# Two-layer hybrid diffusion step on one core: the differential parts' transfers on GpSimd's queue, four of layer 1's first tiles on VectorE, and a planned order chosen by its mean end over varied lengths

## The chip, the core and the metric

One core of one Trainium2 chip runs the kernel. The metric is device time in microseconds (us) of one execution; less is better. TensorE is called PE, VectorE DVE, ScalarE ACT, GpSimd POOL and SyncE SP, as in the profile. SP computes nothing here: it issues most of the DMA transfers. A DMA instruction can also stand in ACT's or POOL's own stream. Each engine carries out its own stream strictly in order, so an instruction that waits holds everything behind it on that engine.

## The reference

A trunk of two layers is applied to 128 context tokens and 256 latent tokens with the same weights. Cut to what matters:

```python
def _mixer_front(x, mod, lp):
    h = _rms(x, lp['g_mix']) * (1.0 + mod[1]) + mod[0]
    cq, ckv, krope, na_q, na_k, na_v, df_q, df_k, df_v = _split_in(h @ lp['w_in'])
    ...
def _diff_attend(q, k, v, lp, lam_init):          # 4 heads of two 32-wide halves
    s1 = q[..., :32] @ k[..., :32].T * scale; s2 = q[..., 32:] @ k[..., 32:].T * scale
    p = softmax(s1) - lam * softmax(s2)
    return _rms(p @ v, lp['g_df_sub']) * (1.0 - lam_init)
def _finish(x, o_mla, o_na, o_df, mod, lp):
    x = x + mod[2] * (concat(o_mla, o_na, o_df) @ lp['w_out'])
    h = _rms(x, lp['g_ffn']) * (1.0 + mod[4]) + mod[3]
    return x + mod[5] * ((silu(h @ lp['w_gate']) * (h @ lp['w_up'])) @ lp['w_down'])
```

`mod` is `silu(cond) @ w_mod + b_mod`, six rows of 1024 for each kind of token. D_MODEL is 1024, the inner width of the last block (the FFN) 2816. Everything is float32.

## The kernel before, in words

**Tiling.** The 384 tokens stand as columns: `xT` is 8 tiles of 128 features by 384 tokens. Float32 accuracy comes from splitting each operand into a high and a low part: `split_hi` (ACT, line 291, tile `wh`) and `split_lo` (DVE, line 297, tile `wl`) make the two parts of a weight block, and `mm3` (lines 363 to 365) runs three PE matmuls for each product. A weight block arrives by a DMA on SP into one of three `raw` buffers (lines 281 and 318).

**Stages.** Each layer has a planned stage (adaLN, norm, input projection `g1`, the three attentions, and the first part of the output projection) and then a plain stage (rest of the output projection and the FFN), where PE gets weight after weight. Between the layers stands a short norm. In the planned stage, the gate rows of `mod` are made beside the attention: `ModSet.load` (line 404) fetches 1 MB of `w_mod` into a `raw` buffer by SP, and `ModSet.mm` (line 414, tile `m`) multiplies it on PE.

**First tiles.** At the start of a layer the 8 feature tiles are normalised: `norm_mul` (DVE, line 552, tile `nt`), `norm_aff` (line 560: two instructions, latent and context tokens) on POOL for the tiles `k` in `POOLK[l]` and else on DVE, `norm_hi` (ACT, line 556, `hh`) and `norm_lo` (DVE, line 564, `hl`). The input projection needs `hh` and `hl` tile by tile.

**Differential heads.** `done_d(p)` takes a 128-token block of a pair of heads: squares, a sum, `rsqrt` on POOL (lines 583 and 584), scaling, rotation (tile `dfo`), a PE transposition (line 1344), and the high and low part in `hs`. `away` (line 1354) writes `hs` to the DRAM tensor `parts`, one DMA of 512 rows of 512 bytes. When the three blocks of a pair are there, `spread` (line 1398) in `df_unit(h)` reads them back for head `h` in eight DMAs of 32 partitions each, in the order of parts that the split product needs, into the tiles `qu` and `ku`. The score matmuls (line 1083) of that head need all eight. So a layer has 6 `away` and 4 `spread`, and all 12 and 64 of these DMAs stand in SP's stream. The neighbourhood heads have a POOL instruction too: a MEMSET (line 1106) of the unused columns of the tile `e`, which the PE transposition (line 1050) of `e` waits for.

**What sets the order.** In the planned stage nothing is ordered by hand. `Plan.add` records tasks with an engine, a cost in us, predecessors, buffers and a priority; `Plan.order` plays them through on these costs and starts on each engine the ready task of best priority. `Plan.best` tries `ORDERS` sets of disturbed priorities, keeps the one whose last task ends first, and the tasks are written to the engines' streams in order of their start. A task on the engine `"dma"` is one in SP's stream, with `LAG` added until its data are there. The plain stage is written in program order.

Of the kernel before, what the change touches and what calls it, by code (L numbers as in the profile page):

```python
# [12 lines left out]
F32 = mybir.dt.float32  # L13
# [5 lines left out]
P = 128  # L19
DM = 1024  # L20
KD = DM // P
NT = 384
# [14 lines left out]
OUT_EARLY = 3  # L37
BUB = (1, 2, 3)
AHEAD = 1
POOLK = ((1, 3, 5, 7), (0, 2, 3, 4, 5, 6, 7))  # L40
PARTS = 4
PARAM = (28, 11)
LAG = 2.8
# [10 lines left out]

WARMUP = (18, 0.43, 16)

ORDERS, STIR = 300, 3.0
CYCLE = 'zszstzt'
WARM = 1
PRT, PRO = (-4.0, -1.1)  # L60
# [24 lines left out]
class Task:  # L85
    def __init__(self, eng, dur, fn, take, prio, ready, lag=0.0):
        self.eng, self.dur, self.fn, self.take, self.prio, self.ready, self.lag = eng, dur, fn, take, prio, ready, lag
        self.need, self.then, self.frees, self.users, self.held, self.start, self.dense = 0, [], [], 0, [], None, 0


class Plan:
# [5 lines left out]
    def __init__(self, room, dense, warm):  # L97
        self.room, self.dense, self.tasks, self.warm = dict(room), dense, [], warm

    def add(self, eng, dur, fn, after=(), take=(), frees=(), prio=0.0, ready=0.0):  # L100
        t = Task(eng, dur, fn, take, prio, ready, LAG if eng == 'dma' else 0.0)
        self.tasks.append(t)
        for a in after:
            if a is not None:
                a.then.append(t)
                t.need += 1
        for h in frees:
            h.users += 1
            t.frees.append(h)
        return t  # L110

    def best(self):

        tasks, room, dense = self.tasks, dict(self.room), self.dense
        was = [(t.need, t.users, t.ready) for t in tasks]

        def run(prios):
            for t, (t.need, t.users, t.ready), t.prio in zip(tasks, was, prios):
                t.held = []
            self.room, self.dense = dict(room), dense  # L120
            return self.order()
        draw = random.Random(0)
        base = [t.prio for t in tasks]
        free = [i for i, t in enumerate(tasks) if t.dur and t.eng != "room"]
        best = list(base)
        run(best)
        end = self.end
        for _ in range(ORDERS):
            p = list(best)
            for i in draw.sample(free, draw.choice((1, 2, 4, 8, 16, 40))):  # L130
                p[i] = base[i] + draw.gauss(0, STIR if draw.random() < 0.8 else 5 * STIR)
            try:
                run(p)
            except AssertionError:
                continue
            if self.end <= end:
                end, best = self.end, p
        return run(best)

    def fit(self, t):  # L140

# [10 lines left out]
    def order(self):  # L152
        events, free, now, n = [], {}, 0.0, 0
        ready = {}
        window, busy, warm = 0, {i: WINDOW for i in range(WARM)} if self.warm else {}, self.warm
        for i, t in enumerate(self.tasks):
            t.key = (t.prio, i)
            free[t.eng] = 0.0
            if not t.need:
                ready.setdefault(t.eng, []).append(t)  # L160
        left = len(self.tasks)
        while left:
            for e in free:
                while free[e] <= now:
                    for t in sorted((t for t in ready.get(e, ()) if t.ready <= now), key=lambda t: t.key):
                        got = self.fit(t)
                        if got is not None:
                            break
                    else:
                        break  # L170
                    ready[e].remove(t)
                    for r in got:
                        self.room[r] -= 1
                    dur = t.dur
# [12 lines left out]
                    t.held, t.start = got, now  # L187
                    free[e] = now + dur
                    n += 1
                    if t.lag:  # L190
                        heapq.heappush(events, (now + dur, -n, t, "wake"))
                    heapq.heappush(events, (now + dur + t.lag, n, t, "done"))
                    heapq.heappush(events, (now + dur + t.lag + self.HOP, n, t, "free"))
            times = [x.ready for l in ready.values() for x in l if x.ready > now]
            if events:
                times.append(events[0][0])
            assert times, [(t.eng, t.take, t.prio, t.fn.__qualname__.split(".")[-1]) for l in ready.values() for t in l][:20]
            now = max(now, min(times))
            while events and events[0][0] <= now:
                _, _, t, what = heapq.heappop(events)  # L200
                if what == "done":
                    left -= 1
                    self.end = now
                    for u in t.then:
                        u.need -= 1
                        u.ready = max(u.ready, now + (0.0 if u.eng == t.eng else self.HOPS.get((t.eng, u.eng), self.HOP)))
                        if not u.need:
                            ready.setdefault(u.eng, []).append(u)
                    self.dense -= t.dense
                elif what == "free":  # L210
                    for h in t.frees:
                        h.users -= 1
                        if not h.users:
                            for r in h.held:
                                self.room[r] += 1
        return sorted(self.tasks, key=lambda t: t.start)


@with_exitstack
def trunk(ctx: ExitStack, tc, xT_d, cv_d, crow_d, pcol_d, prow_d, cache_d, dfk_d, rope_d, bias_d, ident_d,  # L220
# [439 lines left out]
    for l in range(DEPTH):  # L660
# [141 lines left out]
            parts = [None]  # L802
        for k in range(KD):
            x = {}
            a = add(DVE, 0.47, lambda k=k, x=x: x.update(t=norm_mul(k, nst["row"][:, :NT])), after=[bcs], take=("row",), frees=[bcs], prio=URGENT / 2 + k)
            on_pool = k in POOLK[l]
            b = add(POOL if on_pool else DVE, 1.08 if on_pool else 0.6, lambda k=k, x=x, e=nc.gpsimd if on_pool else nc.vector: norm_aff(l, k, x["t"], e),
                    after=[a, parts[k * len(parts) // KD]], prio=NORMP + k)
            b = add(ACT, 0.42, lambda k=k, x=x: norm_hi(k, x["t"], hh), after=[b], prio=NORMP + k)
            hready[k] = add(DVE, 0.47, lambda k=k, x=x: norm_lo(k, x["t"], hh, hl), after=[b], frees=[a], prio=NORMP + k)  # L810

        def weights(key, lead=None, prio=-1000.0, pairs=None):

# [8 lines left out]
            elif lead is None:  # L822
                n = rs[0] * rs[1]
                if pairs:
                    lead = add(DMA, 2.95 / 4096 * n, lambda: w_raw(rk, src, rs, 0), take=("raw", "graw"), prio=pairs[0])
                    lead.mate = add(DMA, 2.95 / 4096 * n, lambda: w_raw(rk, src, rs, 1), after=[lead], prio=pairs[1])
                else:
                    lead = add(DMA, 2.95 / 2048 * n, lambda: w_raw(rk, src, rs), take=("raw", "graw"), prio=5.0 + len(plan.tasks))
            n = shape[0] * shape[1]
# [467 lines left out]
        def done_d(p):  # L1297
            hd = slice(2 * p, 2 * p + 2)

            def done(t, z, unit, room):  # L1300
# [50 lines left out]
                    nc.vector.tensor_tensor(x["hs"][:, 1], x["pt"], x["hs"][:, 0].bitcast(F32), op=ALU.subtract)  # L1351

                def away():
                    nc.sync.dma_start(parts_d[p][:, :, :, t * P:(t + 1) * P], x["hs"].bitcast(F32))
                pr = PDD
                a = add(ACT, 0.27, copy, after=[unit], take=("tok",), frees=[room], prio=URGENT / 2)
                vd_ready[p].append(add(ACT, 0.17, vals, after=[unit], frees=[room], prio=URGENT / 2))
# [9 lines left out]
                g = add(PE, 0.23, turn, after=[f], take=("t",), frees=[f], prio=pr)  # L1367
                u = add(ACT, 0.3, high, after=[g], take=("hs",), frees=[g], prio=pr)
                v = add(DVE, 0.33, low, after=[u], frees=[g], prio=pr)
                df_ready[p][t] = add(DMA, 0.7, away, after=[v], frees=[u], prio=pr)  # L1370
            return done

        du = {}
# [1 line left out]
        def df_unit(h, after, pr):  # L1375
# [17 lines left out]
            def spread():  # L1393

                src = parts_d[h // 2][64 * (h % 2):64 * (h % 2) + 64]
                for i, order in enumerate(((0, 1, 1, 0), (0, 0, 1, 1))):
                    for j, w in enumerate(order):
                        nc.sync.dma_start(du[h][i][32 * j:32 * j + 32, :, (0, P)[i]:(0, P)[i] + NT].bitcast(F32),
                                          src[:, w, i].rearrange("(a r) t -> r a t", a=2))
# [422 lines left out]
```

## Time and profile before

| | |
|---|---|
| median of 3 runs | 1003.67 us (1001.21 to 1004.65) |
| the profiled execution | 1002.43 us, of which the span from first to last instruction is 1000.6 us |
| PE busy | 981.8 us (98%) |
| DVE, ACT, POOL busy | 710.2, 492.9, 153.5 us |
| layer 0 planned stage | from 0 to about 240 us |
| layer 0 plain stage | to about 514 us |
| layer 1 planned stage | about 516 to 720 us |
| layer 1 plain stage | to the end |

How to read it: PE is the engine that matters. "Busy" counts a matmul from start to end, and matmuls overlap, so the places where PE's time is lost are looked for as idle time of PE in stretches of the span, as waits of PE, and in the chain that ended last. The granted TensorE clock is given as a share of full speed.

### The profile page before, as it was taken

The numbers are of one execution on the slowest core, as the hardware profiler recorded it, in microseconds if no ns is written. First come the engines' busy times: TensorE is split into PE (matmuls) and PEld (weight loads), VectorE is DVE, ScalarE is ACT, GpSimd is POOL, SyncE is SP. The second block draws the span as 40 slices with busy tenths as digits, with TensorE's granted clock in tenths as the row PEclk, the third lists the DMA queues.
The fourth block names the chain that finished last, engine by engine and source line by source line (L and its number), as shares of the span: only waits on it lengthen the run. The fifth ranks groups of instructions, "written<-read, shape, count | busy, mean of one in ns | idle before, by whom it ended". The sixth has DMA issues, their size and how long they took to land.

```text
span 1000.6 us, 16452 instructions
## 1 busy us (share of the span) xinstructions
PE 981.8 (98%) x6002; PEld 920.6 (92%) x6002; DVE 710.2 (71%) x1625; ACT 492.9 (49%) x1121; POOL 153.5 (15%) x239
## 2 busy tenths in 40 slices
PE   8999998999999999999999999999999999999998
PEld 7877777999999999999978877889999999999998
DVE  4678876986999999964356887788789655553332
ACT  3366776875433333333326666786653344332221
POOL 2165211201000010100015621230010000000000
PEclk9999999999999999999999999999999999999999
DMA  9858665336666657684462365431765434334450
GB/s 358 334 185 259 215 195 175 109 111 232 201 220 193 228 184 227 200 284 133 134 207 86 109 193 155 137 122 55 253 207 167 132 115 138 102 112 124 137 153 26
DMA packets 139664, 172.84 MB, mean 173 GB/s; under 512 B 6337, under 2 KB 118593, under 8 KB 137281
## 3 DMA queue, kind: packets, MB, share of 16 engines
q1 hardware_dynamic: 131168, 143.38, 45.2%
q0 software_dynamic: 6832, 27.77, 8.1%
q8 instruction: 47, 0.77, 0.3%
q10 hardware_dynamic: 1584, 0.66, 0.2%
q14 instruction: 33, 0.26, 0.1%
HBM read 165.59 MB, written 6.19 MB: 172 GB/s over the span
## 4 chain that ended last, share of the span: by engine, by line
PE 89%; ACT 3%; DMA 2%; DVE 2%; POOL 2%; issue 1%; SPq 0%; ACTq 0%; DVEq 0%; POOLq 0%
PE z L363 13%; PE z L364 13%; PE z L365 13%; PE t L363 6%; PE t L364 6%; PE t L365 6%; PE s L363 6%; PE s L364 6%; PE s L365 6%; PE s L1083 3%; PE m L414 2%; PE t L1050 2%; DMA raw<-in_w_mod 2%; PE t L1191 1%; POOL nt L560 1%; PE s L957 1%
## 5 line engine op out<-in xcount | busy, mean ns | idle before, releaser
L291 ACT ACTIVATE wh<-raw 128x768 fp32r<-128x768 f32 (+3 forms) x224 | 203.3, 909 | 363.5 <-PE z L364 136.0
L297 DVE TENSOR_TENSOR wl<-raw,wh 128x768 fp32r<-128x768 f32 (+3 forms) x224 | 232.5, 1038 | 113.2 <-ACT wh L291 112.2
L363 PE MATMUL z<-fh,wh 128*128 128x386 f32 x304 | 103.2, 339 | 0.0
L364 PE MATMUL z<-fl,wh 128*128 128x386 f32 x304 | 103.0, 339 | 0.0
L365 PE MATMUL z<-fh,wl 128*128 128x386 f32 x304 | 102.6, 338 | 0.0
L486 DVE CUSTOM_DVE_ANT_0 sums<-wt,sums,pcol 128x1024 f32<-128x1024 f32 x80 | 102.3, 1278 | 0.3 <-DVE small L1654 0.3
L363 PE MATMUL z<-wh,hh 128*128 128x384 f32 (+1 forms) x264 | 102.1, 387 | 0.3 <-ACT tok L876 0.3
L365 PE MATMUL z<-wh,hl 128*128 128x384 f32 (+1 forms) x264 | 90.3, 342 | 1.4 <-DVE hl L564 1.4
L364 PE MATMUL z<-wl,hh 128*128 128x384 f32 (+1 forms) x264 | 90.1, 341 | 0.0
L584 POOL TENSOR_TENSOR small<-small,mhalf 128x4 f32<-128x4 f32 (+4 forms) x58 | 72.7, 1254 | 4.8
L363 PE MATMUL s<-fh,wh 128*128 128x386 f32 x200 | 68.2, 341 | 0.0
L363 PE MATMUL t<-fh,wh 128*128 128x386 f32 x200 | 68.1, 341 | 0.0
L364 PE MATMUL s<-fl,wh 128*128 128x386 f32 x200 | 67.8, 339 | 0.0
L364 PE MATMUL t<-fl,wh 128*128 128x386 f32 x200 | 67.8, 339 | 0.0
L365 PE MATMUL t<-fh,wl 128*128 128x386 f32 x200 | 67.5, 338 | 0.0
L365 PE MATMUL s<-fh,wl 128*128 128x386 f32 x200 | 67.5, 338 | 0.0
L1109 ACT ACTIVATE e<-s,small 128x384 f32<-128x384 f32 (+2 forms) x110 | 54.4, 500 | 14.5 <-DVE small L1094 13.0
L480 POOL DMA_DIRECT2D wt<-in_w_modT x40 | 21.6, 540 | 245.7 <-DVE mod L486 190.0
L364 PEld LDWEIGHTS z<-fl,wh 128*128 128x128 f32 x304 | 57.5, 189 | 0.0
L365 PEld LDWEIGHTS z<-fh,wl 128*128 128x128 f32 x304 | 57.3, 189 | 0.0
L363 PEld LDWEIGHTS z<-fh,wh 128*128 128x128 f32 x304 | 57.2, 188 | 0.0
L363 PEld LDWEIGHTS z<-wh,hh 128*128 128x128 f32 x264 | 50.0, 189 | 6.1 <-issue 2.0
(292 smaller groups left out, 2343.3 us busy)
## 6 DMA issues: line engine op xcount, KB each, us to landing
raw<-in_w_gate SPq DMA_DIRECT2D x22, 1024.0 KB, 6.0
raw<-in_w_up SPq DMA_DIRECT2D x22, 1024.0 KB, 5.4
raw<-in_w_down SPq DMA_DIRECT2D x32, 704.0 KB, 4.7
wt<-in_w_modT POOLq DMA_DIRECT2D x40, 512.0 KB, 4.2
raw<-in_w_mod SPq DMA_DIRECT2D x16, 1024.0 KB, 5.2
raw<-in_w_in SPq DMA_DIRECT2D x40, 384.0 KB, 4.3
raw<-in_w_out SPq DMA_DIRECT2D x8, 640.0 KB, 3.9
qu<-in_w_mod SPq DMA_DIRECT2D x8, 512.0 KB, 7.3
```

Of the source, the lines that this page charges most:

```text
L291: nc.scalar.activation(hi, src, AF.Copy)
L297: nc.vector.tensor_tensor(lo, src, hi.bitcast(F32), op=ALU.subtract)
L363: nc.tensor.matmul(out, sh, mh, start=first, stop=False)
L364: nc.tensor.matmul(out, sh, ml, start=False, stop=False)
L365: nc.tensor.matmul(out, sl, mh, start=False, stop=last)
L414: nc.tensor.matmul(self.pm[32 * g:32 * g + 32, :n], sv[:, kb + k, :], w[g // self.per][:, k, i * n:(i + 1) * n], start=(kb + k == 0), stop ...
L480: nc.gpsimd.dma_start(self.w[:, self.loaded % 3], w_modT[l, c * P:(c + 1) * P])
L486: nc.vector.tensor_tensor_reduce(self.junk, self.w[:, self.n % 3], self.s[:, v], 1.0, pcol[l][:, PC_BMOD + c:PC_BMOD + c + 1], ALU.mult, A ...
L584: nc.gpsimd.tensor_tensor(out, t[:, :n], mhalf[:, :n], op=ALU.pow)
L1050: nc.tensor.transpose(pt[:, b, :], x, ident)
L1083: nc.tensor.matmul(ps[:, i, :], q, k, start=True, stop=True)
L1109: nc.scalar.activation(x["e"][i], ps[:, j, :], AF.Exp, bias=x["mx"][:, i:i + 1], scale=-1.0 if bias else 1.0, accum_out=x["su"][:, i:i + 1])
```

## The change

1. `away` and `spread` are issued by `nc.gpsimd.dma_start` and so stand in POOL's stream. In the plan they are tasks of an engine of their own, `"pooldma"`, with the costs that they had (0.7 and 2.3 us, and `LAG`); the engine `"pool"`, on which `rsqrt` and the others are planned, is not held by them.
2. `POOLK` goes from (1, 3, 5, 7) and (0, 2, 3, 4, 5, 6, 7) to (3, 5, 7) and (2, 4, 6, 7): one tile of layer 0 and three of layer 1 go to DVE, which then does 5 of 8 in layer 0 and 4 of 8 in layer 1.
3. The plan's costs of the first tiles are raised (POOL's `norm_aff` from 1.08 to 1.85).
4. `Plan.best` chooses by the mean end over 5 draws of lengths (each engine's costs varied by `BIAS`, lags by 20%, hops lengthened), with the order and the handing on of buffers kept as planned; it tries 700 sets in place of 300. In layer 0, priorities of the first DMA tasks are not disturbed.

The matmuls, splits, transfers and their sizes are the same ones; no arithmetic is added or left out.

```diff
-POOLK = ((1, 3, 5, 7), (0, 2, 3, 4, 5, 6, 7))
+POOLK = ((3, 5, 7), (2, 4, 6, 7))
...
-ORDERS, STIR = 300, 3.0
+ORDERS, STIR = 700, 3.0
+DRAWS, HOPS_MORE, DMA_ENGINE = 5, 0.04, "dma"
+BIAS = {"pe": (0.0, 0.02), "act": (0.03, 0.12), "dve": (0.03, 0.12), "pool": (0.05, 0.25), "dma": (0.05, 0.2), "pooldma": (0.05, 0.2)}
...
-        t = Task(eng, dur, fn, take, prio, ready, LAG if eng == 'dma' else 0.0)
+        t = Task(eng, dur, fn, take, prio, ready, LAG if eng in ('dma', 'pooldma') else 0.0)
...
+        def mean(work):
+            total = 0.0
+            for d, more in zip(lengths, hops):
+                end, last = [0.0] * len(tasks), {}
+                for t in work:
+                    at = max(t.first, last.get(t.eng, 0.0))
+                    for p, hop in t.before:
+                        at = max(at, end[p.index] + (hop + more[t.index] if hop else 0.0))
...
+                total += max(end)
+            return total / len(lengths)
...
-        run(best)
-        end = self.end
+        end = mean(run(best))
...
-            if self.end <= end:
-                end, best = self.end, p
+            if now <= end:
+                end, best = now, p
...
-            b = add(POOL if on_pool else DVE, 1.08 if on_pool else 0.6, lambda ...
+            b = add(POOL if on_pool else DVE, 1.85 if on_pool else 0.68, lambda ...
...
                 def away():
-                    nc.sync.dma_start(parts_d[p][:, :, :, t * P:(t + 1) * P], x["hs"].bitcast(F32))
+                    nc.gpsimd.dma_start(parts_d[p][:, :, :, t * P:(t + 1) * P], x["hs"].bitcast(F32))
...
-                df_ready[p][t] = add(DMA, 0.7, away, after=[v], frees=[u], prio=pr)
+                df_ready[p][t] = add("pooldma", 0.7, away, after=[v], frees=[u], prio=pr)
...
-                        nc.sync.dma_start(du[h][i][32 * j:32 * j + 32, :, (0, P)[i]:(0, P)[i] + NT].bitcast(F32),
+                        nc.gpsimd.dma_start(du[h][i][32 * j:32 * j + 32, :, (0, P)[i]:(0, P)[i] + NT].bitcast(F32),
...
-            d = add(DMA, 2.3, spread, after=[a] + [df_ready[h // 2][t] for t in range(3)], prio=pr)
+            d = add("pooldma", 2.3, spread, after=[a] + [df_ready[h // 2][t] for t in range(3)], prio=pr)
```

The streams differ nearly everywhere in the planned stages, and three places matter below. In the rows, a number in a tile's name counts allocations in the order of the program, so it serves as a common clock over the engines; lines after the change are 41 to 44 higher (`spread` is line 1442, `away` 1398, `ModSet.load` 445, `rsqrt` 624 and 625, the MEMSET 1150, `norm_aff` 601).

Place B, in layer 0, around the third spread. SP's stream before, with two spreads and then loads; `raw` from `in_w_mod` is the gate weights:

```order
L404 DMA raw_1874<-in_w_mod 128x2x1024
L1384 DMA tok_1918<-in_dfk 32x256 x4
L1384 DMA tok_1940<-in_dfk 32x256 x4
L1398 DMA qu_1916<-parts_137 32x2x384 x4
L1398 DMA ku_1917<-parts_137 32x2x384 x4
L1398 DMA qu_1938<-parts_136 32x2x384 x4
L1398 DMA ku_1939<-parts_136 32x2x384 x4
L1246 DMA vn_2058<-in_cache 128x256
L1146 DMA bias_2069<-in_bias 128x576
L404 DMA raw_2079<-in_w_mod 128x2x1024
```

SP's stream after, at the same loads:

```order
L445 DMA raw_1846<-in_w_mod 128x2x1024
L1428 DMA tok_1958<-in_dfk 32x256 x4
L445 DMA raw_1987<-in_w_mod 128x2x1024
L1190 DMA bias_2036<-in_bias 128x576
L359 DMA raw_2051<-in_w_in 128x768 x2
```

The sixteen DMAs of two spreads no longer stand ahead of the last gate weights. POOL's stream after, at this place, holds one of those spreads (the other was moved further ahead):

```order
L624 TENSOR_SCALAR small_1704<-small_1690 128x3
L625 TENSOR_TENSOR small_1691<-small_1704,mhalf 128x3
L1150 MEMSET e_2002 128x96
L1442 DMA qu_1956<-parts_136 32x2x384 x4
L1442 DMA ku_1957<-parts_136 32x2x384 x4
L1150 MEMSET e_2045 128x96
L1150 MEMSET e_2077 128x96
L1150 MEMSET e_2083 128x96
L624 TENSOR_SCALAR small_2123<-small_2103 128x4
```

The eight DMAs now stand between POOL's MEMSETs.

The start of layer 1. POOL's stream before (every `nt` is a first tile, with one row for the latent and one for the context tokens; after these four, three more follow in the same way):

```order
L560 TENSOR_SCALAR nt_5859<-nt_5859,aff_105,mod_103 128x256
L560 TENSOR_SCALAR nt_5859<-nt_5859,aff_105,mod_103 128x128
L560 TENSOR_SCALAR nt_5866<-nt_5866,aff_105,mod_103 128x256
L560 TENSOR_SCALAR nt_5866<-nt_5866,aff_105,mod_103 128x128
L560 TENSOR_SCALAR nt_5893<-nt_5893,aff_105,mod_103 128x256
L560 TENSOR_SCALAR nt_5893<-nt_5893,aff_105,mod_103 128x128
L560 TENSOR_SCALAR nt_5906<-nt_5906,aff_105,mod_103 128x256
L560 TENSOR_SCALAR nt_5906<-nt_5906,aff_105,mod_103 128x128
```

POOL's stream after:

```order
L601 TENSOR_SCALAR nt_5878<-nt_5878,aff_105,mod_103 128x256
L601 TENSOR_SCALAR nt_5878<-nt_5878,aff_105,mod_103 128x128
L601 TENSOR_SCALAR nt_5912<-nt_5912,aff_105,mod_103 128x256
L601 TENSOR_SCALAR nt_5912<-nt_5912,aff_105,mod_103 128x128
L755 TENSOR_SCALAR mskr_5841<-small_5929 128x1
L601 TENSOR_SCALAR nt_5921<-nt_5921,aff_105,mod_103 128x256
L601 TENSOR_SCALAR nt_5921<-nt_5921,aff_105,mod_103 128x128
L601 TENSOR_SCALAR nt_5925<-nt_5925,aff_105,mod_103 128x256
L601 TENSOR_SCALAR nt_5925<-nt_5925,aff_105,mod_103 128x128
L624 TENSOR_SCALAR small_5984<-small_5964,mskr_5841 128x6
```

Four tiles are left on POOL; the other three stand in DVE's stream.

Place C, in layer 1, around its first spread. POOL's stream before:

```order
L583 TENSOR_SCALAR small_6527<-small_6504 128x8
L584 TENSOR_TENSOR small_6505<-small_6527,mhalf 128x8
L583 TENSOR_SCALAR small_6645<-small_6618 128x8
L584 TENSOR_TENSOR small_6619<-small_6645,mhalf 128x8
L583 TENSOR_SCALAR small_6709<-small_6676 128x8
L584 TENSOR_TENSOR small_6677<-small_6709,mhalf 128x8
```

POOL's stream after:

```order
L1398 DMA parts_5849<-hs_6614 512x1x128
L624 TENSOR_SCALAR small_6649<-small_6621 128x8
L625 TENSOR_TENSOR small_6622<-small_6649,mhalf 128x8
L624 TENSOR_SCALAR small_6687<-small_6653 128x8
L625 TENSOR_TENSOR small_6654<-small_6687,mhalf 128x8
L1442 DMA qu_6367<-parts_5849 32x2x384 x4
L1442 DMA ku_6368<-parts_5849 32x2x384 x4
L624 TENSOR_SCALAR small_6770<-small_6707 128x8
L625 TENSOR_TENSOR small_6708<-small_6770,mhalf 128x8
```

A spread that waits for three `parts` now stands ahead of a `rsqrt` (`small_6770`) that the second pair of heads needs.

More of the change, by code (lines that the diff above doesn't have):

```diff
@@ L88, in __init__ @@
         self.need, self.then, self.frees, self.users, self.held, self.start, self.dense = 0, [], [], 0, [], None, 0
+        self.settled, self.last, self.waits = False, [], []
 class Plan:
@@ L98, in __init__ @@
         self.room, self.dense, self.tasks, self.warm = dict(room), dense, [], warm
+        self.settled, self.given = 0, {}
     def add(self, eng, dur, fn, after=(), take=(), frees=(), prio=0.0, ready=0.0):
-        t = Task(eng, dur, fn, take, prio, ready, LAG if eng == 'dma' else 0.0)
+        t = Task(eng, dur, fn, take, prio, ready, LAG if eng in ('dma', 'pooldma') else 0.0)
         self.tasks.append(t)
@@ L115, in best @@
         was = [(t.need, t.users, t.ready) for t in tasks]
+        draw = random.Random(0)
+        for i, t in enumerate(tasks):
+            t.index, t.before = i, []
+        for t in tasks:
+            for u in t.then:
+                u.before.append((t, 0.0 if u.eng == t.eng else self.HOPS.get((t.eng, u.eng), self.HOP)))
+        lengths = [[t.dur * max(0.7, 1 + draw.gauss(*BIAS.get(t.eng, (0, 0)))) + t.lag * max(0.5, 1 + draw.gauss(0, 0.2)) for t in tasks]
+                   for _ in range(DRAWS)]
+        hops = [[draw.expovariate(1 / HOPS_MORE) for _ in tasks] for _ in range(DRAWS)]
         def run(prios):
             for t, (t.need, t.users, t.ready), t.prio in zip(tasks, was, prios):
-                t.held = []
+                t.held, t.waits = [], []
             self.room, self.dense = dict(room), dense
+            self.given = {}
             return self.order()
-        draw = random.Random(0)
+        def mean(work):
[6 more added lines that the diff above has]
+                        at = max(at, end[p.index] + (hop + more[t.index] if hop else 0.0))
+                    for p in t.waits:
+                        at = max(at, end[p.index] + (self.HOP if p.eng != t.eng else 0.0))
+                    end[t.index] = at + d[t.index]
+                    if t.eng != "room":
+                        last[t.eng] = at + d[t.index] - t.lag if t.lag else end[t.index]
+                total += max(end)
+            return total / len(lengths)
+        for t, (_, _, t.first) in zip(tasks, was):
+            pass
         base = [t.prio for t in tasks]
-        free = [i for i, t in enumerate(tasks) if t.dur and t.eng != "room"]
+        free = [i for i, t in enumerate(tasks) if t.dur and t.eng != "room" and not (t.settled or i < self.settled and t.eng == DMA_ENGINE)]
         best = list(base)
-        run(best)
-        end = self.end
+        end = mean(run(best))
         for _ in range(ORDERS):
@@ L132, in best @@
             try:
-                run(p)
+                now = mean(run(p))
             except AssertionError:
                 continue
-            if self.end <= end:
-                end, best = self.end, p
-        return run(best)
+            if now <= end:
+                end, best = now, p
+        work = run(best)
+        self.expected = end
+        return work
     def fit(self, t):
@@ L173, in order @@
                         self.room[r] -= 1
+                        if self.given.get(r):
+                            t.waits.extend(self.given[r].pop(0))
                     dur = t.dur
@@ L186, in order @@
                             a = c
-                    t.held, t.start = got, now
+                    t.held, t.start, t.last = got, now, []
                     free[e] = now + dur
@@ L212, in order @@
                         h.users -= 1
+                        h.last = [u for u in h.last if u.eng != t.eng] + [t]
                         if not h.users:
@@ L215, in order @@
                                 self.room[r] += 1
+                                self.given.setdefault(r, []).append(h.last)
         return sorted(self.tasks, key=lambda t: t.start)
@@ L804, in trunk @@
             x = {}
-            a = add(DVE, 0.47, lambda k=k, x=x: x.update(t=norm_mul(k, nst["row"][:, :NT])), after=[bcs], take=("row",), frees=[bcs], prio=URGENT / 2 + k)
+            a = add(DVE, 0.52, lambda k=k, x=x: x.update(t=norm_mul(k, nst["row"][:, :NT])), after=[bcs], take=("row",), frees=[bcs], prio=URGENT / 2 + k)
             on_pool = k in POOLK[l]
-            b = add(POOL if on_pool else DVE, 1.08 if on_pool else 0.6, lambda k=k, x=x, e=nc.gpsimd if on_pool else nc.vector: norm_aff(l, k, x["t"], e),
+            b = add(POOL if on_pool else DVE, 1.85 if on_pool else 0.68, lambda k=k, x=x, e=nc.gpsimd if on_pool else nc.vector: norm_aff(l, k, x["t"], e),
                     after=[a, parts[k * len(parts) // KD]], prio=NORMP + k)
-            b = add(ACT, 0.42, lambda k=k, x=x: norm_hi(k, x["t"], hh), after=[b], prio=NORMP + k)
-            hready[k] = add(DVE, 0.47, lambda k=k, x=x: norm_lo(k, x["t"], hh, hl), after=[b], frees=[a], prio=NORMP + k)
+            b = add(ACT, 0.5, lambda k=k, x=x: norm_hi(k, x["t"], hh), after=[b], prio=NORMP + k)
+            hready[k] = add(DVE, 0.55, lambda k=k, x=x: norm_lo(k, x["t"], hh, hl), after=[b], frees=[a], prio=NORMP + k)
+        plan.settled = len(plan.tasks) if l == 0 else 0
         def weights(key, lead=None, prio=-1000.0, pairs=None):
@@ L826, in weights @@
                     lead.mate = add(DMA, 2.95 / 4096 * n, lambda: w_raw(rk, src, rs, 1), after=[lead], prio=pairs[1])
+                    lead.settled = lead.mate.settled = True
                 else:
```

## The prediction

> **What bounds the kernel now.** I read the clock first, then the busy time by stretches of the span.
>
> ```profile
> core 0: 1000.6 us, clock 0.998
> core 0: us, PE busy (x) PEld busy (x) DVE busy (x) ACT busy (x) POOL busy (x), PEclk, DMA share, GB/s
> 0.00:20.00 20.00, 17.30 (x170) 16.15 (x171) 7.61 (x22) 7.31 (x14) 3.39 (x9) 1.00 0.91 348
> ...
> 140.00:160.00 20.00, 16.25 (x116) 12.84 (x116) 12.52 (x40) 12.29 (x41) 5.75 (x11) 0.91 0.62 181
> ...
> 240.00:500.00 260.00, 260.00 (x1481) 258.64 (x1480) 210.65 (x392) 99.82 (x149) 19.87 (x35) 1.00 0.64 202
> ...
> 520.00:540.00 20.00, 17.62 (x94) 13.77 (x87) 14.69 (x32) 8.59 (x24) 13.97 (x20) 1.00 0.53 187
> ...
> 580.00:600.00 20.00, 18.97 (x119) 15.54 (x117) 16.80 (x50) 14.13 (x43) 5.89 (x6) 1.00 0.77 223
> 600.00:620.00 20.00, 18.30 (x120) 14.74 (x119) 15.30 (x45) 14.12 (x46) 3.50 (x6) 1.00 0.56 170
> 620.00:720.00 100.00, 99.46 (x630) 92.37 (x629) 81.75 (x224) 73.39 (x213) 18.66 (x40) 1.00 0.41 126
> ...
> sum 1000.60, PE 981.84 PEld 920.62 DVE 710.16 ACT 492.87 POOL 153.55; mean PE 70.13 PEld 65.76 DVE 50.73 ACT 35.20 POOL 10.97
> ```
>
> PE is idle for 1000.60 - 981.84 = 18.8 us. The plain stages (240:500 is one) have none of it, and no matmul is removed, so only idle time and lost clock can be won. Three places lie within reach of this change: 140:160 with 3.75 us and a clock of 0.91 (20 x 0.09 = 1.8 us more), 520:540 with 2.4, and 580:620 with 1.0 + 1.7 = 2.7 us. Together that is 10.7. The start (0:20) waits for its first loads, which stay.
>
> Next, PE's longest wait, the chain that ended last at the first place (start, length, what), and SP's stream there:
>
> ```profile
> PE m L414 <- DMA raw<-in_w_mod: 5.1, 2, 3.7
> 147.48 1.15 SPq L1398
> 149.63 6.54 DMA raw<-in_w_mod
> 156.21 1.87 PE m L414 x16
> 140.49 1.78 SPq L1398 DMA_DIRECT2D qu<-parts  x4
> 142.31 1.84 SPq L1398 DMA_DIRECT2D ku<-parts  x4
> 144.25 1.78 SPq L1398 DMA_DIRECT2D qu<-parts  x4
> 146.08 2.56 SPq L1398 DMA_DIRECT2D ku<-parts  x4
> 149.63 0.43 SPq L404 DMA_DIRECT2D raw<-in_w_mod  x1
> ```
>
> Two spreads held SP from 140.49 to 148.64, so the gate weights (L404) were issued only at 149.63, landed 6.54 us later, and PE stood still for them. The second place, in the chain:
>
> ```profile
> 581.85 4.23 DMA qu<-parts
> ...
> 593.00 8.58 DMA raw<-in_w_mod
> 601.62 1.07 PE m L414 x8
> ```
>
> A spread's landing is on the chain, and then gate weights again. At the third place the chain runs over POOL's first tiles:
>
> ```profile
> 520.71 3.13 POOL nt L560 x3
> ...
> 528.00 4.83 POOL nt L560 x6
> ```
>
> **What is removed.** *Gate weights, layer 0.* After the change no spread stands ahead of `raw_1987` on SP, so its issue need not wait the 1.78 + 2.56 us of the nearer spread, and more by the other one. That is over the gap of 3.75 us; it closes, and with it the clock loss behind it: 5.5 us. Should the transfer stay slow, part of it stays, so I take 5.0, between 1 and 5.5. *Layer 1, 580:620.* SP is free of `away` and spread, and the load of the last gate weights moves ahead. Of 2.7 us I take 2.0, between 0 and 2.7, since other waits lie near. *First tiles of layer 1.* Three tiles go from POOL to DVE:
>
> ```profile
> L560 POOL TENSOR_SCALAR nt<-nt,aff,mod 128x128 f32<-128x128 f32 x11 | 9.9, 902 | 0.0
> L560 POOL TENSOR_SCALAR nt<-nt,aff,mod 128x256 f32<-128x256 f32 x11 | 7.6, 687 | 29.6 <-DVE aff L460 25.2 <-DVE nt L552 4.3
> L560 DVE TENSOR_SCALAR nt<-nt,aff,mod x10: 340/378/416, 20.0 to 521.3; 128x256 f32<-128x256 f32 x5, 128x128 f32<-128x128 f32 x5
> ```
>
> A tile costs POOL 0.69 + 0.90 = 1.59 us: seven take 11.1, four 6.4. On DVE a tile costs 2 x 0.38 = 0.76, so three add 2.3 us to 14.7 busy of 20. They fit, though DVE is then nearly the last one there. Of PE's 2.4 idle us I take 1.7, between 0 and 2.4. The tile moved in layer 0 lies beside the loads of the start: nothing. The gains sum to 8.7 us.
>
> **What is added.** POOL gets 12 `away` and 64 spread DMAs. No row shows such a DMA on POOL. The nearest are POOL's own loads of `w_modT` (128 pieces each) and the same transfers on SP, each with its time from issue to landing below it:
>
> ```profile
> L480 POOL DMA_DIRECT2D wt<-in_w_modT x40: 527/530/656, 232.0 to 760.5; - x40
> DMA to landing us min/median/max: 3.7/4.2/7.2
> L1398 SPq DMA_DIRECT2D qu<-parts x32: 323/424/1273, 94.6 to 646.3; - x32
> DMA to landing us min/median/max: 2.0/2.3/4.8
> L584 POOL TENSOR_TENSOR small<-small,mhalf 128x8 f32<-128x8 f32 x12 | 21.9, 1821 | 1.0
> L583 POOL TENSOR_SCALAR small<-small 128x8 f32<-128x8 f32 x12 | 4.0, 330 | 22.5 <-DVE small L1359 22.1
> ```
>
> I take 0.53 us each, POOL's median, since the engine decides more than the shape does; the bounds are 0.32, SP's least, and 2.1 for an `away`, if 512 pieces cost four times 128. A spread then holds POOL for 8 x 0.53 = 4.2 us, where the plan holds it for nothing. Its last DMA lands 2.3 to 4.2 us later, so a head's scores can start 6.5 to 8.4 us after the spread does. Whatever POOL has behind the spread starts 4.2 us late. The cover for both is the PE work written between, priced by these pieces of the chain:
>
> ```profile
> 135.09 0.18 PE z L363
> 139.10 0.49 PE s L1083 x2
> 139.59 0.33 PE t L1050 x3
> 142.91 1.45 PE t L1191 x12
> ```
>
> - A, first spread of layer 0: up to its scores PE has 30 weight matmuls (30 x 0.18 = 5.4), 11 transpositions (1.2) and 4 gate matmuls (0.5, at 1.87/16 each): 7.1. With an `away` of 0.53 ahead the need is 7.0 to 8.9. Short by 0 to 1.8; I take 0.5.
> - B, third spread of layer 0: 12 weight matmuls (2.1), 11 transpositions (1.2), 3 scores (0.7), 8 of L1191's and its neighbour's kind (0.9): 4.9. Short by 1.6 to 3.5; I take 2.0, nearer the short landing of SP's row, as the size is the same. The MEMSETs behind this spread are needed about as late and wait inside the same stall.
> - C, first spread of layer 1: the spread waits for its third part, covered by two `rsqrt` of 0.33 + 1.82 = 2.15 each. Behind it the next `rsqrt` is late: 4.2 + 2.15 + about 0.9 for two DVE operations = 7.3, against 30 x 0.18 + 10 x 0.11 + 3 x 0.25 = 7.3 of PE work up to the transposition that needs it. Nothing to 1.7 (a dear `away`); I take 0.5.
> - D, third spread of layer 1: about 6.7 of cover against 6.5 to 8.4; I take 0.4, between 0 and 1.7. The other four spreads have 15 us and more: nothing.
>
> Sum of losses 3.4 us, from 1.6 to 8.7. The new order as such has no price in any row. The stretch 620:720 idles 0.54 us with the old one, so there is nothing to win there, and I give it 0 with 2.5 either way.
>
> **The sum.** 8.7 - 3.4 = 5.3 us of gain. The profiled execution took 1002.43 us (span 1000.6), and would take 997.1; it lies 1.2 below the median of the three, 1003.67, from which the sum gives 998.4. I predict between the two, 997.7.
>
> One page speaks against the gain. The Trainium skill, "DMA: Bandwidth & Descriptors", section "Issuing engines are not separate DMA queues", says that DMAs from any engine share the same 16 DMA engines, and that another issuing engine saves only the time of issue. By that rule the sum would be that of the rival "no change", below. The trace agrees in part: issue time alone, 140.49 to 148.64, is what stood in SP's way.
>
> **The rivals.**
> - *No change.* The gate weights land late not for SP but since all transfers share the DMA engines: one took 6.54 us, another 8.58. The spreads now run beside the loads in place of ahead of them. Then the first gap stays, gains are 0 + 1 + 1.7, losses 3.4: 1002.43 + 0.7 = 1003.1. Against it: PE's stall is shorter than the time for which SP was held.
> - *Slower: POOL's DMAs cost much more than 0.53.* Each of the four short covers lengthens by 8 times the excess; the gain is gone where 3.4 + 32 (x - 0.53) = 8.7, at x = 0.70. If each DMA first waits out one DVE operation like this one,
>
> ```profile
> L1119 DVE TENSOR_SCALAR e<-e,small 128x384 f32<-128x384 f32 x24 | 10.1, 420 | 0.8
> ```
>
>   x is 0.95, the losses 16.8, and the time 1002.43 + 8.1 = 1010.5. Against it: POOL's 40 loads never took over 656 ns though DVE was busy 210.65 of 260 us. The Trainium skill, "SBUF — State Buffer", section "Who interferes with whom", states this rule: a DVE operation in a two-port mode, which tensor_scalar can enter, blocks GpSimd for its whole length, and so its writing of descriptors. No row here shows it for a DMA on POOL.
> - *Faster than forecast.* Covers suffice everywhere and all three places close: 1002.43 - 10.7 = 991.7, with the order's share down to 990.
>
> **How the numbers follow.** About 0.3%, 3 us, is what a measurement of this kernel can tell from no change. My forecast (994 to 1000.6) has 0.48, faster still 0.14, no change (1000.7 to 1006.7) 0.25, slower by POOL's price 0.13. So faster 0.62, same 0.25, slower 0.13. The range from 991 to 1005 leaves out most of the slower case and the end of the best.
>
> **What would show it.** In the changed kernel's profile: PE has no wait for `raw<-in_w_mod` over 1 us, and the clock of 140:160 is 1.00. POOL's DMAs (lines 1398 and 1442) take near 0.53 us each and some 40 us in all. PE idles at the scores (line 1127) after a third spread, up to 3 us. In 516 to 540 us PE's idle time falls below 1 us. The prediction is wrong if POOL's DMAs take over 0.7 us, if `rsqrt` (lines 624, 625) becomes what PE's transpositions wait for, or if the gate weights still land late.

## The result, and the profile after

The changed kernel takes 1013.96 us (median of three, 1011.58 to 1014.34) where the kernel before takes 1003.67: 1.0103 times as long, interval 1.0085 to 1.0121. The forecast was 997.7, a gain. The profiled execution is the median one, 1013.96 us with a span of 1012.2, so it stands beside the 1000.6 of before.

First the clock, then busy time by stretches of the changed kernel, with the columns as before; two stretches of the kernel before that were not shown follow it:

```profile
core 0: 1012.2 us, clock 0.993
0.00:20.00 20.00, 17.09 (x161) 15.39 (x162) 6.76 (x17) 6.88 (x14) 3.40 (x9) 0.91 0.92 348
...
40.00:140.00 100.00, 93.58 (x579) 74.38 (x581) 67.40 (x190) 57.46 (x168) 52.98 (x70) 0.97 0.65 212
140.00:160.00 20.00, 19.25 (x139) 13.97 (x128) 14.87 (x45) 15.67 (x49) 5.72 (x14) 1.00 0.63 185
...
500.00:540.00 40.00, 37.59 (x212) 32.02 (x211) 22.52 (x46) 12.22 (x20) 5.27 (x7) 0.96 0.58 191
540.00:620.00 80.00, 76.57 (x445) 66.52 (x444) 59.11 (x164) 51.67 (x149) 42.38 (x55) 1.00 0.40 126
620.00:720.00 100.00, 96.44 (x618) 86.21 (x617) 80.02 (x228) 74.41 (x229) 32.32 (x65) 1.00 0.42 122
...
sum 1012.20, PE 987.37 PEld 922.95 DVE 711.21 ACT 492.25 POOL 191.12; mean PE 123.42 PEld 115.37 DVE 88.90 ACT 61.53 POOL 23.89
```

```profile
40.00:140.00 100.00, 99.97 (x654) 78.41 (x643) 74.18 (x208) 65.77 (x194) 37.64 (x46) 1.00 0.69 228
...
500.00:540.00 40.00, 36.63 (x209) 30.24 (x209) 22.69 (x47) 14.51 (x32) 14.84 (x21) 1.00 0.52 175
540.00:620.00 80.00, 76.72 (x457) 64.90 (x456) 63.75 (x178) 55.49 (x166) 30.97 (x39) 1.00 0.46 141
```

The span grew by 11.6 us: PE's idle time from 18.8 to 24.8, and PE's busy time by 5.5, at an unchanged count of matmuls. The busy part is the clock: 20 x 0.09 + 100 x 0.03 + 40 x 0.04 = 6.4 us lost by it, against 1.8 before; 1.8 of the 6.4 lie at the start, ahead of every `away` and spread. The place that the change aimed at did mend: 140:160 has 0.75 idle us in place of 3.75, and a clock of 1.00. But 40:140, which had no idle time, has 6.4 us of it and 3 us of lost clock, and 620:720 went from 0.5 to 3.6.

What PE waits for in the changed kernel, and what POOL does ahead of the 2.4 and the 1.8 us of waiting, both near 104 us (start, length, what):

```profile
PE t L984 <- DVE tok L1026: 2.4, 1, 2.4
...
PE s L1127 <- DMA ku<-parts: 1.8, 1, 1.8
...
PE m L455 <- DMA raw<-in_w_mod: 0.5, 2, 0.3
DVE tok L1024 <- POOL small L625: 4.3, 1, 4.3
```

```profile
94.75 0.25 POOL L624 TENSOR_SCALAR small<-small 128x8 f32<-128x8 f32 x1 [1.28 <-DVE small L1403]
...
96.70 0.75 POOL L1398 DMA_DIRECT2D parts<-hs  x1
97.44 2.17 POOL L1442 DMA_DIRECT2D qu<-parts  x4
99.59 1.60 POOL L1442 DMA_DIRECT2D ku<-parts  x3
102.48 0.54 POOL L1442 DMA_DIRECT2D ku<-parts  x1 [1.29 <-DMA parts<-hs]
103.08 0.24 POOL L624 TENSOR_SCALAR small<-small 128x6 f32<-128x6 f32 x1
...
105.75 1.73 POOL L625 TENSOR_TENSOR small<-small,mhalf 128x8 f32<-128x8 f32 x1
```

Gate weights are waited for 0.3 us at most, so SP is out of the way. In its place stands POOL: one `away`, then a spread, whose last transfer waits 1.29 us for the part that this `away` sent, and behind them two `rsqrt`. VectorE waits 4.3 us for the first one, PE for VectorE, and then for the spread's own landing. On the chain stand that part's 5.50 us to its landing and 5.80 us from the last transfer's issue to its own:

```profile
96.70 5.50 DMA parts<-hs
...
102.48 5.80 DMA ku<-parts
...
108.41 0.98 PE s L1127 x2
```

At 622 us a spread and an `rsqrt` behind it stand on the chain, and PE waits 1.3 us:

```profile
624.57 2.12 POOL ku L1442 x4
...
627.08 1.05 POOL small L625
```

### The profile page after: what moved, and what is told of

It is laid out like the page before. It is cut to its first block, busy times and chain, and to the rows that moved or that the text cites. A ratio compares the mean times of both kernels' runs of the same rounds, so it can differ in the third digit from the quotient of the medians.

```text
span 1012.2 us, 16505 instructions
## 1 busy us (share of the span) xinstructions
PE 987.4 (98%) x6002; PEld 923.0 (91%) x6002; DVE 711.2 (70%) x1633; ACT 492.3 (49%) x1121; POOL 191.1 (19%) x307
## 4 chain that ended last, share of the span: by engine, by line
PE 83%; DVE 4%; ACT 4%; POOL 3%; DMA 3%; issue 2%; ACTq 0%; DVEq 0%; POOLq 0%
PE z L404 12%; PE z L406 12%; PE z L405 12%; PE t L404 6%; PE t L405 6%; PE t L406 6%; PE s L404 5%; PE s L405 5%; PE s L406 5%; PE s L1127 2%; PE t L1235 2%; PE t L1094 2%; PE m L455 1%; DMA parts<-hs 1%; POOL small L625 1%
```

## The experiments

Two theories stood against each other. *Queue*: the transfers hold POOL, and `rsqrt` behind them comes late. *Order*: the new search writes a worse order, whoever issues. Each run beside the kernel before on the same chip (whose median was 1003.4 to 1004.4 us):

| run | away, spread on | order from | median us | ratio to before, interval |
|---|---|---|---|---|
| changed kernel | POOL, POOL | new plan, seed 0 | 1013.96 | 1.0103, 1.0085 to 1.0121 |
| e1_sp_issue | SP, SP | the changed kernel's | 1004.63 | 1.0023, 1.0009 to 1.0037 |
| e10_away_only | POOL, SP | the changed kernel's | 1005.96 | 1.0023, 1.0009 to 1.0037 |
| e7_spread_only | SP, POOL | the changed kernel's | 1007.72 | 1.0040, 1.0024 to 1.0056 |
| e14_half | POOL, half | the changed kernel's | 1005.92 | 1.0019, 1.0006 to 1.0032 |
| e5_pool_held | SP, SP, POOL held | the changed kernel's | 1008.51 | 1.0049, 1.0033 to 1.0066 |
| e2_pool_issue | POOL, POOL | the kernel before's | 1015.78 | 1.0126, 1.0101 to 1.0150 |
| e8_after_seed | POOL, POOL | new plan, seed 1 | 1003.85 | 0.9999, 0.9988 to 1.0010 |
| e16_after_seed2 | POOL, POOL | new plan, seed 2 | 1015.19 | 1.0112, 1.0090 to 1.0134 |
| e3_plan_sp | SP, SP | new plan, seed 0 | 999.93 | 0.9964, 0.9948 to 0.9979 |
| e9_plansp_seed | SP, SP | new plan, seed 1 | 996.42 | 0.9929, 0.9914 to 0.9944 |
| e17_plansp_seed2 | SP, SP | new plan, seed 2 | 1000.42 | 0.9962, 0.9950 to 0.9975 |
| e4_booked | POOL, POOL | POOL booked, seed 0 | 1002.49 | 0.9989, 0.9979 to 0.9999 |
| e13_booked_seed | POOL, POOL | POOL booked, seed 1 | 1007.73 | 1.0045, 1.0028 to 1.0061 |
| e11_search_only | SP, SP | new search, old tiles, seed 0 | 999.73 | 0.9967, 0.9953 to 0.9982 |
| e15_search_seed | SP, SP | new search, old tiles, seed 1 | 997.68 | 0.9940, 0.9922 to 0.9958 |
| e12_tiles_only | SP, SP | old search, new tiles | 1005.34 | 1.0031, 1.0017 to 1.0046 |

**Swap the queue alone, in both orders.** e1 takes the changed kernel's order and issues on SP:

```diff
-                    nc.gpsimd.dma_start(parts_d[p]...
+                    nc.sync.dma_start(parts_d[p]...
-                        nc.gpsimd.dma_start(du[h][i]...
+                        nc.sync.dma_start(du[h][i]...
```

> The changed kernel's order, unaltered, with the 12 away and 64 spread transfers issued on SP in place of POOL. Queue theory (the spread's eight DMAs, 4.3 us, stand on POOL ahead of rsqrt, lines 624/625, and PE waits for what rsqrt feeds): POOL's rsqrt no longer waits behind them, so the 2.4 + 1.8 us of PE idle near 104 us and the 6.8 us of half clock behind it go; 1001 to 1006 us, with some new wait for gate weights on SP. Order theory (the new search writes a worse order, whatever queue issues the transfers): 1010 to 1014 us.

e2 makes the opposite edit of the same two lines in the kernel before, whose order stays.

> The kernel before in its own order, with only the issuing queue of away and spread changed from SP to POOL; the plan still books them on SP's queue. Queue theory: POOL's rsqrt and MEMSETs come 4.3 us late behind each spread, 1008 to 1016 us, though the 3.75 us wait for gate weights at 152 us is gone. Order theory: with the order of before only the gains remain, 996 to 1002 us.

The queue theory's ranges hold on both sides: 9.3 us go when the changed kernel's transfers leave POOL, and 1.26% come when those of before go there. The order has a share of its own, though: in e1 40:140 still idles 3.7 us, at a clock of 1.00, and the whole is 0.23% slower than before. In e2, what PE waits for, and the chain through its first and its third spread:

```profile
PE s L1083 <- DMA ku<-parts: 4.9, 1, 4.9
PE t L1344 <- DVE dfo L1334: 4.6, 2, 4.2
PE t L1344 <- DVE dfo L1336: 2.7, 2, 2.5
```

```profile
98.80 6.00 DMA parts<-hs
...
105.08 0.54 POOL ku L1398
...
106.03 1.68 POOL small L584
...
109.76 0.66 PE t L1344 x2
```

```profile
155.14 1.59 POOL ku L1398 x3
156.73 7.32 DMA ku<-parts
...
164.14 0.98 PE s L1083 x2
```

The first spread stops at the head of POOL's queue until its part has landed, and the `rsqrt` behind it makes PE wait 4.2 us. At the third it is the spread's own landing, 7.32 us. No wait for gate weights is left in e2's list either, so what the change aimed at works there too, and is outweighed.

**Leave the transfers on SP, plan and all.** e3 is the change without its transfers; e9 and e17 are the same with other seeds of the search, and e8 and e16 are the changed kernel with those seeds (`random.Random(1)` and `random.Random(2)`).

```diff
-                df_ready[p][t] = add("pooldma", 0.7, away, ...
+                df_ready[p][t] = add(DMA, 0.7, away, ...
-            d = add("pooldma", 2.3, spread, ...
+            d = add(DMA, 2.3, spread, ...
```

> The change without its transfers: away and spread stay on SP and are planned there; the new first tiles (three and four on POOL), the new costs and the search by mean end over five draws stay, so it writes an order of its own. Queue theory: 996 to 1003 us. Order theory: 1008 to 1014 us.

> The changed kernel with another random seed (1 for 0) for its search, so another order from the same costs, still blind to POOL's 4.4 us. Queue theory: an order that doesn't know of the time stands rsqrt behind some spread again, 1007 to 1018 us. Chance theory (this one order was unlucky): 998 to 1005 us.

> Run e3 (new search, costs and first tiles, transfers on SP and planned there) with the other seed. If the 999.93 us of e3 come from the search, the costs and the tiles: 997 to 1003 us again. If they came from a lucky order: 1003 to 1010 us.

> The changed kernel with a third seed (2). If the queue costs in any order: 1002 to 1015 us, 4 us or more above e17. If the loss at seeds 0 and 1 belonged to those orders: within 3 us of e17.

> Run e3 (the change with its transfers left on SP and planned there) with the third seed. By e3 and e9: 996 to 1001 us, below the kernel before. If those two were lucky: 1002 us or more.

On SP every seed beats the kernel before; on POOL none of the three does. Seed by seed, POOL is 14.0, 7.4 and 14.8 us slower; the two orders of a seed differ too, since the plan knows where the transfers stand. For e8 the queue theory's range (1007 to 1018) missed and the chance theory's (998 to 1005) held. Its order meets only one such stall, though a long one: POOL idles 2.84 us with a spread at the head of its queue, then issues it (585.53 to 589.86), and PE waits 5.8 us for what the `rsqrt` behind it feeds:

```profile
PE t L1388 <- DVE small L1158: 5.8, 1, 5.8
```

```profile
585.53 2.23 POOL L1442 DMA_DIRECT2D qu<-parts  x4 [2.84 <-PE t L1388]
587.74 2.12 POOL L1442 DMA_DIRECT2D ku<-parts  x4
589.93 0.24 POOL L624 TENSOR_SCALAR small<-small 128x8 f32<-128x8 f32 x1
```

So luck of the order is worth up to 11.3 us on POOL (1003.85 to 1015.19) and 4.0 on SP, and with each seed the version on POOL is the slower one. e9 ended 0.6 us under its range.

**Hold POOL without a DMA.** e5 is e1 with work of the same length on POOL in each spread's place:

```diff
+                for n in (8, 8, 3):
+                    nc.gpsimd.tensor_tensor(scratch[:, :n], ones[:, :n], mhalf[:, :n], op=ALU.pow)
```

> Run e1 (the changed kernel's order, transfers issued on SP) with three pow operations of 8, 8 and 3 columns on a scratch tile put into POOL's stream where each spread stood: about 4.3 us of POOL's time, by the rows of 128x8 and 128x3 (1.8 and 0.9 us), and no DMA on POOL. Holding theory (what costs is that POOL is busy for 4.3 us ahead of rsqrt): most of the loss comes back, 1009 to 1014 us, with PE waiting behind rsqrt near 104 us. Landing theory (what costs is that the spread's last DMA is issued and lands later from POOL): 1003 to 1006 us, as e1's 1004.63.

e7 makes the first of e1's two edits alone, so the spreads stay on POOL.

> The changed kernel with only the 12 away transfers put back on SP, the 64 of the spreads still on POOL, its order unaltered. If the spreads carry the loss: 1009 to 1014 us. If the away transfers carry it, which took POOL 0.75 us each where 0.53 was forecast: 1003 to 1007 us.

POOL's timeline at the first spread, in e5 and then in e1:

```profile
93.18 0.25 POOL L625 TENSOR_SCALAR small<-small 128x8 f32<-128x8 f32 x1 [1.28 <-DVE small L1404]
...
95.14 4.34 POOL L1442 TENSOR_TENSOR scratch<-ones,mhalf 128x8 f32<-128x8 f32 x3
...
102.23 1.73 POOL L626 TENSOR_TENSOR small<-small,mhalf 128x8 f32<-128x8 f32 x1
```

```profile
93.44 0.25 POOL L624 TENSOR_SCALAR small<-small 128x8 f32<-128x8 f32 x1 [1.28 <-DVE small L1403]
...
100.08 1.73 POOL L625 TENSOR_TENSOR small<-small,mhalf 128x8 f32<-128x8 f32 x1
```

From the first of these rows to the last `rsqrt` pass 6.6 us in e1, 9.1 in e5, and 11.0 in the changed kernel. e5 loses 3.9 us on e1's median and e7, with the real spreads on POOL, 3.1 (3.0 and 2.2 when each is taken beside the kernel before on its own chip). As far as these runs tell, holding POOL costs no less than the spreads do, and a later landing need not be called on for this part. The sign is visible at 620 us, where e5 and e7 have the same new wait and e1 has none (e5's row; e7's reads 1.3):

```profile
PE t L1310 <- DVE tok L1325: 1.4, 1, 1.4
```

Neither reached the 1009 us that each theory of "all the loss" had asked for, and neither fell into the other range. e5's runs spread from 1005.46 to 1012.56 (its rows are of one at 1006.21), the intervals of e1 and e5 just touch (1.0037, 1.0033) and e7's overlaps e1's more widely, so the medians prove less than the rows do.

**The fourth corner, and half a spread.** e10 makes the second of e1's edits alone, so that only `away` stays on POOL. e14 issues the four `ku` transfers of each spread on SP, and a spread holds POOL for 2.2 us:

```diff
-                        nc.gpsimd.dma_start(du[h][i]...
+                        (nc.gpsimd, nc.sync)[i].dma_start(du[h][i]...
```

> The changed kernel's order with only the 12 away transfers on POOL and the 64 of the spreads back on SP: the fourth corner to e1 (both on SP, 1004.63 us), e7 (only the spreads on POOL, 1007.72) and the changed kernel (both, 1013.96). If the two add up, each at its own price: 1010 to 1012 us. If the away transfers cost only together with the spreads, since a spread at the head of POOL's queue waits for the part that an away on the same queue sent late: 1004 to 1007 us.

> The changed kernel's order with the four qu transfers of each spread on POOL as now and the four ku transfers on SP: a spread holds POOL for 2.2 us in place of 4.3, the away transfers stay on POOL. If the cost grows with the time held: halfway between e10 (1005.96 us, no spread on POOL) and the changed kernel (1013.96), 1008.5 to 1011.5 us. If it sets in at a point that 2.2 us doesn't reach: 1004 to 1007.5 us. If one transfer at the head of POOL's queue is enough to stall it: 1012 to 1015 us.

The loss of `away` alone (e10, 1.3 us on e1's median) and of the spreads alone (e7, 3.1) can hardly be told from nothing: the ratio of e10 is e1's, and e7's interval overlaps it. Together they cost 9.3 us, which is clear of both, so the costs don't add up. Nor can e14 be told from e1. But e14 also takes from POOL the transfer that waits for its part, so it doesn't separate the length of the hold from that stop. The rows of the first spread fit this: PE's waits there are under 2 us as long as the last `rsqrt` comes 9.1 us or less behind the first row (6.6 in e1 and e10, 7.9 in e14, 9.1 in e5 and e7); with `away` (0.75) and the wait for its landing (1.29) in the same queue it comes 2 us later, which is past what PE has to do meanwhile.

**Tell the plan of POOL's time.** e4 books `away` and spread on POOL; e13 is the same with seed 1.

```diff
-            d = add("pooldma", 2.3, spread, ...
+            d = add(POOL, 4.4, spread, ...
+            d.lag = LAG
```

> The changed kernel with away and spread on POOL as now, but booked there in the plan, at the measured 0.75 us and 4.4 us of POOL's own time with the same lag behind; it writes an order of its own. Queue theory: the plan moves rsqrt out of the spread's way, 997 to 1004 us. Order theory: 1010 to 1015 us. A third possibility, that POOL is simply too slow for both: above 1008 us with POOL's rsqrt still what PE waits for.

> Run e4 (away and spread on POOL and booked there) with the other seed, beside e8 (the same, not booked, 1003.85 us) and e9 (on SP, 996.42 us). If knowing POOL's time is enough: 996 to 1000 us. If POOL's 44 us cost something wherever they stand: 1000 to 1005 us, as e4's 1002.49 beside e3's 999.93.

With seed 0 booking wins 11.5 us back; with seed 1 it is 3.9 us worse than not booking, above both ranges expected for it, and gate weights are late again in it (2.6 us). In e4 PE's longest wait, 2.4 us, is for a MEMSET of POOL. Both stay 2.6 and 11.3 us above the same seed on SP. Knowing of the time is not enough. Whether a better search over the booked plan could reach SP's times stays open.

**The rest of the change.** e11 and e15 are e3 and e9 with the old `POOLK` and the old costs of the first tiles, so the new search alone; e12 is the kernel before with the new ones (cut):

```diff
-POOLK = ((1, 3, 5, 7), (0, 2, 3, 4, 5, 6, 7))
+POOLK = ((3, 5, 7), (2, 4, 6, 7))
...
-            b = add(POOL if on_pool else DVE, 1.08 if on_pool else 0.6, lambda ...
+            b = add(POOL if on_pool else DVE, 1.85 if on_pool else 0.68, lambda ...
...
```

> The kernel before with the new search alone (mean end over five draws, 700 orders, buffer hand-over kept): transfers on SP, old first tiles and old costs. If the search makes the gain of e3 and e9: 997 to 1001 us. If the first tiles and their costs make it: 1002 to 1006 us.

> Run e11 (the kernel before with the new search alone) with seed 1, beside e9 (new first tiles and costs as well, same seed, 996.42 us). If the tiles and costs are worth something under the new search: 998 to 1001 us. If they are worth nothing: 995 to 998 us.

> The kernel before with the new first tiles and their costs alone: transfers on SP, old search. If the tiles make the gain of e3 and e9: 997 to 1001 us, and PE's idle time at the first tiles of layer 1 falls below 1 us from 2.4. If the search makes it: 1001 to 1006 us, moved only by the tiles' 1.7 us and by the luck of another order.

The gain belongs to the search: 999.73 us without the tiles, 999.93 with them. With seed 1 it is 997.68 and 996.42, with intervals that overlap, so what the tiles add there is not shown. With the old search e12 is slower by 0.31%, which another order alone can do (4.0 us between seeds on SP). Which part of the new search gains, the mean over draws or the 700 sets in place of 300, was not separated.

**The best version** of these is e9: the change with its transfers left on SP, 996.42 us, 0.71% faster than the kernel before. Its clock, and from its list of PE's waits the first line and the longest for a load of `in_w_mod`:

```profile
core 0: 994.6 us, clock 0.998
PE z L404 <- ACT hh L597: 1.8, 1, 1.8
...
PE m L455 <- DMA ku<-in_w_mod: 0.9, 1, 0.9
```

The list has no wait for `raw<-in_w_mod` of 0.2 us or more, with all 76 transfers on SP: a better order took SP's stall away too. (The `ku<-in_w_mod` of 0.9 us is an earlier load, within the first 90 us.)

## Why the prediction was wrong, step by step

- *Gate weights, layer 0 (5.0 us taken): right.* 140:160 gained 3.0 idle us and 1.8 of clock; the longest wait for them is 0.3. But e9 shows that the queue need not be changed for it.
- *Layer 1, 580 to 620 (2.0): not won.* No wait for gate weights is left there, yet 540:620 idles 3.4 us against 3.3, nearly all of it behind 580. In e1, the same order on SP, 540:620 idles 0.5, so in this order the gain could be had. The prediction had put this down as "other waits lie near" and then took most of the gain all the same.
- *First tiles (1.7): not won.* 500:540 idles 2.4 us in place of 3.4, 1.0 gained, and a half clock piece of 1.7 us there gave it back. 516 to 540 kept 2.4 us of idle time, where the prediction's sign was less than 1.
- *POOL's price of 0.53: right for the spreads, too low for `away`.* Means in the changed kernel:

```profile
L1442 POOL DMA_DIRECT2D qu<-parts x32 | 18.0, 568 | 6.7 <-PE t L1094 3.0 <-issue 2.5 <-PE s L1127 1.1
L1442 POOL DMA_DIRECT2D ku<-parts x32 | 17.2, 548 | 1.3 <-DMA parts<-hs 1.3
L1398 POOL DMA_DIRECT2D parts<-hs x12 | 9.0, 752 | 11.5 <-DVE hs L1395 5.5 <-DVE small L1158 4.8 <-DVE small L1058 1.3
```

  They sum to 44.2 us where "some 40" was forecast. The rival that ended slower named a price above 0.70 for the spreads, and that did not happen; the longest took 0.70 us. The rule of the Trainium skill, "SBUF — State Buffer", section "Who interferes with whom", that a DVE operation in a two-port mode blocks GpSimd, is not seen in the time for which these transfers hold POOL (0.53 to 0.70 us for the spreads); whether it stands behind their longer landings, below, no run separates. The kernel ended on that rival's side by another mechanism.
- *The stalls A to D (3.4): the step that failed, at A.* The order that was priced is the changed kernel's (at C it has an `away`, two `rsqrt` and the spread). Of its four places only A is dear: PE waits 2.4 us behind the `rsqrt` and 1.8 at the scores, 4.2 where 0.5 was taken, and 6.8 us of half clock follow. B, taken at 2.0, shows no wait for its landing, C a wait of 0.8 ahead of its transposition, D none. A was sized by PE's work up to the spread's own scores. The `rsqrt` behind the spread was priced only at C, and the stop of the eighth transfer for its part (1.29 us) nowhere. The landing was mis-sized: 5.80 us, where 2.3 to 4.2 was assumed. From issue to landing the spreads took, in the changed kernel and then in e1, with the same order:

```profile
DMA to landing us min/median/max: 2.2/4.7/8.1
```

```profile
DMA to landing us min/median/max: 2.0/2.7/8.2
```

  In the order of before the median is 2.3 us on SP and 4.5 on POOL (e2), so POOL's row, not SP's, was the nearer one; what makes it longer, no run separates. One of the "other four spreads", the second of layer 1, cost 1.3 us by the `rsqrt` behind it. The prediction had named the sign itself: wrong "if `rsqrt` becomes what PE's transpositions wait for". Which place pays hangs on the order: in e2, with that of before, the first spread of layer 0 costs 4.2 us, the third 4.9 (its landing took 7.32), and the first of layer 1 2.5.
- *No term for the clock behind new stalls.* Each was priced at its own length. The changed kernel lost 4.6 us more by the clock than the kernel before. Of this the 3.0 at 40:140 lie behind A's stalls. The 1.8 at the start and the 1.6 at 500:540 are not shown to be the queue's: e3 and e9, with the transfers on SP, drop at 500:540 too (0.91 and 0.96).
- *The order as such (0, 2.5 either way): too narrow.* One seed or another moves the changed kernel by 11.3 us, and the new search alone is worth 0.33% (e11). That the stretch 620:720 had nothing to win was no reason that the rest hadn't; and it lost 3.0.

By stretches of the two profiled executions, A with its half clock is the largest miss, some 7 us; some 4.6 us of the gains were not won, 620:720 lost 3.0 and the start 2.0.

What the runs price is this. With the order held, the queue costs 9.3 us in the changed kernel's order (against e1) and 12.3 in that of before (e2). The changed kernel lies 14.0 us above e3, so 4.7 of them (e1 against e3) belong to its order, which was planned with the transfers on an engine that holds nobody. In what makes up the 9.3, the hold, the stop for the part and the longer landing, the shares stay open.

The page that the prediction set beside the rival "no change", the Trainium skill's "DMA: Bandwidth & Descriptors", section "Issuing engines are not separate DMA queues", says that another issuing engine saves only the time of issue. Here that time, saved on SP, ended the wait for gate weights at 140:160 (in e2 too, whose order is that of before), and it cost more where it went: SP had it to spare and POOL, with `rsqrt` in its queue, hadn't.

## What to carry to other kernels

Before a transfer moves to an engine that computes, list what stands behind it in that engine's queue and who waits for it, and count the waits of the transfer itself, since they stop the queue too. Price short covers together, not one by one: two additions that alone could hardly be told from nothing cost 9 us here once they shared one cover. And split a change that alters a schedule's search from one that alters the hardware's work, over a few seeds, since here one hid the other's gain.

## What the runs showed of the hardware

The clock drops behind a stretch of some 3.4 us that PE was idle for only in part. Stretches of the changed kernel of some 3.4 us around two such drops (the columns as before):

```profile
103.40:106.80 3.40, 0.83 (x5) 0.28 (x4) 1.97 (x4) 0.16 (x1) 3.22 (x3) 1.00 1.00 314
106.80:113.60 6.80, 5.19 (x18) 5.08 (x19) 3.97 (x8) 2.67 (x7) 1.44 (x2) 0.50 0.63 195
...
530.04:533.45 3.41, 1.99 (x11) 1.10 (x8) 3.37 (x9) 0.52 (x1) 1.33 (x2) 1.00 1.00 349
533.45:536.87 3.42, 3.42 (x12) 3.24 (x11) 3.38 (x9) 1.67 (x5) 0.11 (x2) 0.50 0.88 315
```

Behind a stretch in which PE was busy 0.83 of 3.4 us came 6.8 us of half clock (in the first half of them PE was busy 1.79 us), and behind one with 1.99 of 3.41 busy came 3.4 us. Each 3.4 us costs up to 1.7. The Trainium skill, "TensorE: Matmul & The Clock Gate", section "What's actually happening", speaks of a free-running window of 3413 ns and of a drop after an idle one. The length agrees, but here stretches that were busy for a quarter and for 58% of their time were enough. What share decides isn't settled by these runs.
